# A two-layer network on one core: the scheduler's price for a change of array part, the experts' inputs transposed before their norm, and a twentieth place for weights

## The chip, the cores and the metric

The kernel runs on one core of a Trainium2 chip. The metric is the device time in microseconds, the median over runs of the same program. The engines go by the profile's names: PE (TensorE, with PEld for its weight loads), DVE (VectorE), ACT (ScalarE), POOL (GpSimd), SP (SyncE, which issues the DMAs).

## The reference

One sequence of 256 tokens of width 1024 goes through a first block (mixer and mixture of experts) and a second block of two layers. All is float32. Cut to what matters here:

```
h = rms_norm(x) * (1 + sc_m) + sh_m;  x = x + g_m * hybrid_mixer(h)     # SSD, forgetting attention, conformer
h = rms_norm(x, norm_ffn_g) * (1 + sc_f) + sh_f                          # the experts' inputs
e_logits, p_g = h @ w_re + b_re, softmax(h @ w_rg + b_rg)                # one of 4 groups, two of its 8 experts
y = sum over the two experts e of weight[e] * ((silu(h @ w_gate[e]) * (h @ w_up[e])) @ w_down[e])
x = rms_norm(x + g_f * y, final_norm_g)
for i in 0, 1:                                                           # the second block
    xn = rms_norm(x, norm_pre[i])
    y = rwkv7_time_mix(xn) if i == 0 else diff_attention_mix(xn, k, v)   # a recurrence per head, then attention
    x = x + rms_norm(y, norm_post[i])
    x = x + rms_norm(sigmoid(x @ ple_gate[i]) * (p[i] @ ple_w[i]), ple_norm[i])
```

`sc_f`, `sh_f` and the others are six parts of one modulation vector; `s.modc(n, j)` in the kernel is chunk j of part n, and part 3 is `sh_f`. There are 32 experts, each with 2 MB of gate, 2 MB of up and 2 MB of down weights: 192 MB in all. The recurrence of the time mix is done in chunks of 64 tokens, for which the inverse of a 64x64 triangular matrix is made per head.

## The kernel before

A dense product is made at float32 accuracy from three fast ones (type fp32r): each operand is split into a hi and a lo part, and hi·hi, hi·lo and lo·hi are added in PSUM. Small products and transposes are made in plain float32. A product with at most 64 rows of contraction or 64 output partitions uses a part of the 128x128 array. The diff writes a part as (rows, columns): (128, 128), (64, 64), (64, 128), (128, 64), (32, 32).

The work has three stages. In the mixer (`mixer_streams`, to L1118) and in the second block (`second`, L1524) the order of the instructions is made when the program is built: streams, which are generators that yield one instruction at a time, are merged by `Mux.run` (L317). `Plan` (L146 to 276) keeps for each engine the time at which it comes free, and for each tile the time at which it is ready. `Plan.cost` (L198) prices an instruction, `start` (L194) says when it can begin, `clocked` (L231) counts the work that TensorE is given in slots of 3413 ns and doubles a price where the slot before had little of it; `cool` (L242) says whether the recent work is under `HEAT`, and then `Mux.run` takes an fp32r product if one can go. `enter` (L248) books the instruction taken; there, an fp32r product behind one with at most 64 output partitions is priced 54 ns more. The plan is started anew for the second block (`reset`, L157).

The stage between them, the experts (`experts`, L1334), is ordered by hand: sixteen pairs of experts, the two of a pair in the two halves of the array's columns. For a pair the inputs of the tokens chosen are gathered by products with a 0/1 matrix `P` (`gather`, L1356: 32 products `px` per two pairs, evicted in four pieces of 128x512 by ScalarE and VectorE in turn), then `pgu` (gate and up), `ph` (transposes), `py` (down) and a scatter into `acc`. The weights come in pieces of 1 MB, by DMAs of SP's queue, into a ring of 19 places (`first_weights`, L1137): four of the pool `ring_b`, eleven tiles of their own (`MORE`), four of the pool `ring`. The places are taken from the mixer's memory, so that a load must wait for the mixer's last use of it, and all loads behind it on the queue wait with it. A place comes free again by the products that read it.

What the experts read, `hh` and `hl` (`s.h2`), is made at the end of the mixer. The stream `gather` (L1038, of the same name as the function above) makes `xc` = x * gain and sums squares, and from them the norm `rsq_y` (`s.rms2`, for each token one value on its partition). `tokens` (L1066) spreads the norm over all partitions as `R`, multiplies `xc` with it (eight times, `s.add`, VectorE or GpSimd) and adds `sh_f` (eight times, ScalarE). `turned` (L1080) then transposes `xc`, 128x128 at a time into four banks of PSUM, writes the hi part with ScalarE and the lo part with VectorE. Meanwhile `route` (L1246, tiles `qk`, `slot`, `wt`) chooses the experts, its sums over tokens being products with the triangular matrices `tri` and `stri`. `places` (L1345) makes `P` of `slot`.

In the second block, the names on TensorE are: `pd` dense fp32r products (of `xm`, the mixed inputs, in the time mix), `pi` the 64x64 and 32x32 products of `rwkv_invert` (L2242), `pm` and `pq` the transposes and products around it (`rwkv_inner`, L2123), `pe` those of `rwkv_chunks` (L2298). Eight pairs of heads go through inner, invert and chunks; in the invert each step of a pair is eight `pi` products, a copy on ScalarE, eight `pi` products, a copy and a transpose on VectorE. In the profile, all instructions of the two scheduled stages stand under L72, the helper that issues them.

Of the kernel before, what the change touches and what calls it, by code (L numbers as in the profile page):

```python
# [47 lines left out]
HEAT = 3500, 3550  # L48
# [3 lines left out]
MORE = 11  # L52
# [84 lines left out]
class Plan:  # L137
# [8 lines left out]
    def __init__(s, nc):  # L146
        s.nc = nc
        s.at = {}
        s.use = {}
        s.free = {}  # L150
        s.work, s.past, s.part, s.heat = {}, [], False, HEAT[0]
        s.log = []
        s.cur = None
        for n in ("tensor", "vector", "scalar", "gpsimd", "sync"):
            setattr(s, n, Lane(s, getattr(nc, n), n))

    def reset(s):  # L157

        s.at = {"dma": 0.0, "scalar": 10e3, "gpsimd": 11e3, "tensor": 16e3, "vector": 15.8e3}
        s.use, s.free, s.work, s.past, s.heat = {}, {}, {}, [], HEAT[1]  # L160
# [33 lines left out]
    def start(s, op, lag=0):  # L194
        eng = op.lane.name
        return op.ready if eng == "sync" else max(op.ready + lag * (eng == "tensor"), s.at.get(eng, 0.0))

    def cost(s, op):  # L198
# [4 lines left out]
        if eng == "tensor":  # L203
            if name == "transpose":
                return 109
            if ins[0].dtype == F32R:
                return max(107, n / 2.4) + 2
            m = out.ap[0][1]
            if m > 64:
                return max(214, n * 4 / 2.4 + 4)  # L210
            if s.box(out)[0]:
                return 22 if m <= 32 else 53
            return max(107, n * 4 / 2.4) + 2
# [16 lines left out]

    def clocked(s, start, dur, op):  # L231

        w = int(start / 3413.3)
        n = 1 if op.ins[0].dtype == F32R else 2
        for _, c in op.outs[0].ap[1:]:
            n *= c
        n *= op.ins[0].ap[0][1] / 128 * (dur > 53)
        s.work[w] = s.work.get(w, 0.0) + n
        s.past.append((start, n))
        return dur if s.work.get(w - 1, 0.0) > 3060 else 2 * dur  # L240

    def cool(s, t):  # L242

        while s.past and s.past[0][0] < t - 3413.3:
# [3 lines left out]
    def enter(s, op, r):  # L248
# [6 lines left out]
        else:  # L255
            start = s.start(op)
            if eng == "tensor":

                part = op.outs[0].ap[0][1] <= 64
                dur = s.clocked(start, dur + 54 * (s.part and op.ins[0].dtype == F32R), op)  # L260
                s.part = part
# [22 lines left out]
class Mux:  # L284
# [32 lines left out]
    def run(s):  # L317
        pl = s.plan
        while s.st:
# [10 lines left out]
            can = [(pl.start(o, x.lag), x.rank if o.lane.name == "tensor" else x.side, i, x, o) for i, x in enumerate(s.st) for o in x.head]  # L330
# [13 lines left out]
class K:  # L344
# [65 lines left out]
    def consts(s, tp):  # L410
# [18 lines left out]
        s.tri = cp.tile([128, 256], F32, name="tri")  # L429
# [3 lines left out]
        s.stri = cp.tile([128, 128], F32, name="stri")  # L433
# [39 lines left out]
    def mixer_streams(s, mp):  # L473
# [16 lines left out]
        for i in range(4):  # L490
            t("cu", S, tag=f"cu{i}")
        for i in range(2):
            for q in "hl":
                mp.tile([128, 8 * 268], F32R, name="w" + q, tag=f"w{q}{i}")
        t8 = t("t8", 8)
# [542 lines left out]
        def gather():  # L1038
# [12 lines left out]
            for j in range(NJ):  # L1051
# [3 lines left out]
                       A.activation(sq, xT[:, j], AF.Square)]  # L1055
                for c in range(2):
# [6 lines left out]
            s.pl = pl  # L1063
            done.add("rms")

        def tokens():  # L1066

            yield has("rms")
            tag = yield from s.one()
            R = s.bank(tag, [128, S])  # L1070
            yield from s.spread(s.rms2, R)
            yield A.copy(s.R1, R)
            s.give(tag)
# [6 lines left out]
        def turned(c):  # L1080
            for q in range(2):
                tag = yield from s.one()
                p = s.bank(tag, [128, 512])
                for j in range(4):
                    yield has(("x2", 4 * q + j))
                    yield nc.tensor.transpose(p[:, 128 * j:128 * j + 128], xc[:, 4 * q + j, 128 * c:128 * c + 128],
                                              ident)
                hi, lo = [x[:, c, 512 * q:512 * q + 512] for x in s.h2]
                yield A.copy(hi, p)
# [1612 lines left out]
```

## Time and profile before

| | us |
|---|---|
| median of three runs | 1298.44 (1293.02 to 1301.1) |
| the profiled execution | 1295.23, of which the span from first to last instruction 1293.3 |
| mixer, to the last expert input | 0 to some 221 |
| experts | some 221 to 662 |
| second block | 662 to 1293 |

The views of the trace are: the busy time of each engine; windows, which give the same for a stretch, with TensorE's granted clock (PEclk, 1.00 is 2.4 GHz and 0.50 is 1.2 GHz) and the DMA engines' share; and the timeline of one engine, in which neighbours of one kind stand in one row with their count. In a timeline the length of a row is that of the instructions from issue to end, and overlaps the next row's by the way through the engine: how long a run holds its engine is read from start to start.

### The profile page before, as it was taken

The page shows a single profiled execution, that of the slowest core. Times are in us where ns is not written, and L with a number is a line of the kernel's source. Part 1 is how long each engine was busy: PE and PEld are TensorE (multiplying, and loading weights), DVE is VectorE, ACT ScalarE, POOL GpSimd, SP SyncE. Part 2 cuts the span into 40 slices and gives each one's busy share as a digit, 9 for nine tenths or more (in the row PEclk, how much of TensorE's full clock was granted, in tenths as well). Part 3 has the DMA queues.
Part 4 walks back from the last instruction along what each step waited for, and adds up shares of the span by engine and source line. Part 5 has one row for each costly group of instructions (what it writes and reads, how often), then busy time and mean ns, then how long its engine had stood idle before and what let it go on. Part 6 is the DMA issues. An engine that isn't in the chain of part 4 may idle for free. (4 is left out here: it accounts for less than half of the span.)

```text
span 1293.3 us, 20461 instructions
## 1 busy us (share of the span) xinstructions
PE 1185.9 (92%) x7906; PEld 809.4 (63%) x7906; DVE 660.4 (51%) x1782; ACT 435.3 (34%) x1074; POOL 127.6 (10%) x358
## 2 busy tenths in 40 slices
PE   5999987999999989898986989999999989899896
PEld 3777886344343444444356867877777656888775
DVE  5695766111111111111027952576676677788885
ACT  3564543011110101111024721333344445655543
POOL 1000000000000000000000211222222002022212
PEclk8999996999999999999996975899999999899999
DMA  9658566899999999999983421111212342544422
GB/s 374 276 225 331 217 254 259 335 421 421 420 420 421 420 420 421 420 421 420 420 324 101 143 70 38 38 54 39 70 57 92 129 141 86 170 157 148 141 82 75
DMA packets 52628, 306.14 MB, mean 237 GB/s; under 512 B 5680, under 2 KB 10288, under 8 KB 25392
## 3 DMA queue, kind: packets, MB, share of 16 engines
q1 hardware_dynamic: 52368, 304.67, 60.1%
q8 instruction: 64, 1.05, 0.3%
q14 instruction: 36, 0.29, 0.1%
q0 software_dynamic: 160, 0.13, 0.1%
HBM read 302.55 MB, written 2.10 MB: 236 GB/s over the span
## 5 line engine op out<-in xcount | busy, mean ns | idle before, releaser
L366 PE MATMUL pgu<-w,xe 128*64 128x512 f32 x1024 | 233.0, 595 | 15.6 <-DMA w<-moe 15.6
L366 PEld LDWEIGHTS pgu<-w,xe 128*64 128x64 f32 x1024 | 80.9, 137 | 155.8 <-issue 116.6
L72 PE MATMUL pd<-xm,whl 128*128 128x256 f32 x768 | 149.3, 324 | 5.5 <-ACT xm L72 3.9
L72 DVE TENSOR_TENSOR whl<-raw,whl 128x512 fp32r<-128x512 f32 x192 | 128.4, 683 | 11.0 <-ACT whl L72 10.3
L72 ACT CAST whl<-raw 128x512 fp32r<-128x512 f32 x192 | 111.3, 618 | 40.5 <-PE pd L72 23.7
L72 PEld LDWEIGHTS pd<-xm,whl 128*128 128x128 f32 x768 | 112.9, 207 | 18.5 <-ACT xm L72 4.5
L366 PE MATMUL py<-w,hT 128*64 128x512 f32 (+1 forms) x528 | 116.6, 583 | 7.0 <-ACT hT L1408 7.0
L1433 DVE SCALAR_TENSOR_TENSOR yl<-py,ws,yh 128x512 fp32r<-128x512 f32 (+1 forms) x33 | 24.2, 734 | 123.4 <-ACT yh L1432 123.4
L366 PEld LDWEIGHTS py<-w,hT 128*64 128x64 f32 x528 | 40.7, 137 | 71.4 <-issue 54.7
L1352 POOL TENSOR_TENSOR PW<-P,wt 128x256 f32<-128x256 f32 x16 | 9.9, 617 | 617.7 <-PE pw L1413 213.4
L1432 ACT ACTIVATE yh<-py,ws 128x512 fp32r<-128x512 f32 (+1 forms) x33 | 22.2, 675 | 119.6 <-PE acc L366 66.1
L1398 DVE TENSOR_TENSOR hid<-hid,pgu 128x512 f32<-128x512 f32 x16 | 11.0, 688 | 98.2 <-PE pgu L366 98.1
L1397 DVE SCALAR_TENSOR_TENSOR hid<-hid,pgu 128x512 f32<-128x512 f32 x16 | 11.0, 688 | 96.8 <-ACT hid L1396 96.7
L72 PE MATMUL pd<-hh,whl 128*128 128x256 f32 x384 | 59.0, 295 | 1.4 <-ACT whl L72 0.8
L72 PE MATMUL pd<-xx,whl 128*128 128x256 f32 x384 | 54.2, 287 | 1.7 <-ACT whl L72 0.9
L72 PEld LDWEIGHTS pd<-hh,whl 128*128 128x128 f32 x384 | 50.6, 194 | 4.8 <-issue 2.6
L72 PE MATMUL pd<-whl,hh 128*128 128x512 f32 x192 | 52.4, 407 | 1.1 <-ACT hh L72 1.1
L72 PEld LDWEIGHTS pd<-xx,whl 128*128 128x128 f32 x384 | 48.9, 192 | 3.5 <-ACT whl L72 1.2
L72 PE MATMUL a<-hl,wh 128*128 128x256 f32 x160 | 47.1, 294 | 1.5 <-DVE hl L72 1.5
L72 PE MATMUL a<-hh,wh 128*128 128x256 f32 x160 | 46.8, 292 | 0.6 <-DVE x L72 0.6
L72 PE MATMUL a<-hh,wl 128*128 128x256 f32 x160 | 46.5, 291 | 0.0
L72 DVE TENSOR_TENSOR wl<-w,wh 128x512 fp32r<-128x512 f32 (+1 forms) x60 | 39.3, 692 | 10.5 <-ACT wh L72 10.4
(506 smaller groups left out, 2230.3 us busy)
## 6 DMA issues: line engine op xcount, KB each, us to landing
w<-moe SPq DMA_DIRECT2D x190, 1024.0 KB, 19.8
w<-ada SPq DMA_DIRECT2D x12, 2048.0 KB, 11.8
raw<-awin SPq DMA_DIRECT2D x32, 512.0 KB, 3.4
raw<-bwin SPq DMA_DIRECT2D x32, 512.0 KB, 3.5
w<-win SPq DMA_DIRECT2D x5, 2048.0 KB, 12.0
raw<-pleg SPq DMA_DIRECT2D x16, 512.0 KB, 3.3
w<-wout SPq DMA_DIRECT2D x2, 2048.0 KB, 8.6
raw<-awout SPq DMA_DIRECT2D x8, 512.0 KB, 3.4
```

Of the source, the lines that this page charges most:

```text
L72: r = s.fn(*s.a, **s.k)
L366: return s.nc.tensor.matmul(out, lhsT=lhsT, rhs=rhs, start=first, stop=last, **kw)
L1352: G.tensor_tensor(PW.rearrange(four, e=2), P[:, :, o:o + 128].bitcast(F32).rearrange(four, e=2), wt[:, :, 2 * i:2 * i + 2, None].to_broadc ...
L1397: V.scalar_tensor_tensor(hid, hid, 1.0, pgu[0], op0=OP.add, op1=OP.mult)
L1398: V.tensor_tensor(hid, hid, pgu[1], op=OP.mult)
L1432: A.activation(y[0], p, AF.Copy, scale=ws)
L1433: V.scalar_tensor_tensor(y[1], p, ws, y[0].bitcast(F32), op0=OP.mult, op1=OP.subtract)
```

## The change

The change has three parts.

The planner. A change between parts of the array is priced (`change`: 95 ns, 138 where little work was booked in the slot before; nothing within a part, and nothing from (64, 128) to (128, 128)) and is part of the time at which a product can start. `come`, by which streams are compared, leaves the price out once the present spell of one kind (fp32r or not) has lasted `LONG`. The prices of the small products and the work booked for them go by part, and `HEAT` is another.

```
-HEAT = 3500, 3550
+SPELL = 3413.3
+WORK = {(128, 128): 3.2, (64, 64): 1.7, (64, 128): 2.2, (128, 64): 1.9, (32, 32): 1.5, (128, 32): 1.0}
+HEAT = 3300, 3300
+LONG = 400, 1400
-MORE = 11
+MORE = 12
...
     def start(s, op, lag=0):
         eng = op.lane.name
-        return op.ready if eng == "sync" else max(op.ready + lag * (eng == "tensor"), s.at.get(eng, 0.0))
+        if eng == "tensor":
+            return max(op.ready + lag, s.at.get(eng, 0.0) + s.change(op))
+        return op.ready if eng == "sync" else max(op.ready, s.at.get(eng, 0.0))
+
+    def come(s, op, lag=0):
+        t = s.start(op, lag)
+        if op.lane.name == "tensor":
+            at = s.at.get("tensor", 0.0)
+            if at - s.since > (LONG[s.whole]):
+                t = max(op.ready + lag, at)
+        return t
...
+    def cold(s, t):
+        return s.work.get(int(t / SPELL) - 1, 0.0) < 2880
+
+    def change(s, op):
+        op = getattr(op, "ops", [op])[0]
+        if s.part is None or s.part == s.form(op) or (s.part, s.form(op)) == ((64, 128), (128, 128)):
+            return 0
+        return 138 if s.cold(s.at.get("tensor", 0.0)) else 95
+
     def clocked(s, start, dur, op):
-        w = int(start / 3413.3)
-        n = 1 if op.ins[0].dtype == F32R else 2
+        part, whole = s.form(op), op.ins[0].dtype == F32R
+        cold = s.cold(start)
+        if cold:
+            dur = 2 * (dur - 11) if whole else 1.9 * dur
+        if whole and part != s.part:
+            dur += 165 if cold else 105
+        n = 1.0 if whole else 1.5 if op.op == "transpose" else WORK[part]
...
-            can = [(pl.start(o, x.lag), x.rank if o.lane.name == "tensor" else x.side, i, x, o) for i, x in enumerate(s.st) for o in x.head]
+            can = [(pl.come(o, x.lag), x.rank if o.lane.name == "tensor" else x.side, i, x, o) for i, x in enumerate(s.st) for o in x.head]
```

The experts' inputs. `tokens` is gone. `turned` transposes `xc` without its norm, as soon as its chunks are made; the norm, which then lies along the partitions, is the scale of the eviction that makes the hi part, and of the one that makes the lo part. `sh_f` is added where the gathered inputs leave PSUM, for which each bank is evicted in two pieces.

```
-        def tokens():
...
-            for j in range(NJ):
-                x = xc[:, j]
-                yield s.add(x, x, s.R1, OP.mult, 150)
-                yield A.activation(x, x, AF.Identity, bias=s.modc(3, j))
-                done.add(("x2", j))
...
+            tags, ps = [], []
+            for q in range(2):
+                yield has(*[("x2", 4 * q + j) for j in range(4)])
+                tags.append((yield from s.one()))
+                ps.append(s.bank(tags[q], [128, 512]))
+                for j in range(4):
+                    yield nc.tensor.transpose(ps[q][:, 128 * j:128 * j + 128], xc[:, 4 * q + j, 128 * c:128 * c + 128],
+                                              ident)
             yield has("rms")
             for q in range(2):
...
+                rs = s.rms2[:, c:c + 1]
+                yield A.activation(hi, ps[q], AF.Copy, scale=rs)
+                yield V.scalar_tensor_tensor(lo, ps[q], rs, hi.bitcast(F32), op0=OP.mult, op1=OP.subtract)
+                s.give(tags[q])
...
-                (V.tensor_copy if q % 2 else A.copy)(xe[:, 2 * q:2 * q + 2], p)
+                for j in range(2):
+                    sh = s.modc(3, 2 * q + j)
+                    if q % 2:
+                        V.tensor_scalar(xe[:, 2 * q + j], p[:, j], sh, None, op0=OP.add)
+                    else:
+                        A.activation(xe[:, 2 * q + j], p[:, j], AF.Identity, bias=sh)
```

The memory. A twelfth tile of its own makes twenty places. For it `stri` and `tri` become one tile `order`, which later holds the weighted matrix `PW`; `hid` and `hT` use the memory of `condp`; and some of the mixer's tiles (`R1`, `xc`, `dg`, `wr36`) are made in another order, so that the last places lie under other tiles than before.

On VectorE, at the end of the mixer, these were the last rows ahead of `P` (`xc` the multiplications by the norm, `qk`, `wt`, `slot`, `cnt` the routing, `hl` the lo parts of the experts' inputs):

```order
L72 TENSOR_TENSOR xc<-xc,R_196 128x256
L72 TENSOR_TENSOR wt<-qk 128x64
L72 SCALAR_TENSOR_TENSOR slot<-x_2271,qk 128x64
L72 TENSOR_TENSOR hl<-x_229,hh 128x512
L72 TENSOR_SCALAR slot<-slot 128x64
L72 TENSOR_TENSOR hl<-x_230,hh 128x512
L72 TENSOR_REDUCE qk<-x_2271 128x1
L72 CAST cnt<-qk 128x1
L72 TENSOR_TENSOR hl<-x_2294,hh 128x512
L72 TENSOR_TENSOR hl<-x_2303,hh 128x512
L1345 TENSOR_TENSOR P<-slot,iot 128x512
```

These are they now, from the first lo part on, and, behind ten more rows of the routing, down to `P`:

```order
L76 SCALAR_TENSOR_TENSOR hl<-x_2216,rsq_y,hh 128x512
L76 SCALAR_TENSOR_TENSOR qk<-qk 128x64
L76 SCALAR_TENSOR_TENSOR hl<-x_2136,rsq_y,hh 128x512
L76 TENSOR_REDUCE qk<-qk 128x8
L76 SCALAR_TENSOR_TENSOR hl<-x_2217,rsq_y,hh 128x512
```

```order
L76 TENSOR_TENSOR wt<-qk 128x64
L76 SCALAR_TENSOR_TENSOR slot<-x_2283,qk 128x64
L76 TENSOR_SCALAR slot<-slot 128x64
L76 TENSOR_REDUCE qk<-x_2283 128x1
L76 CAST cnt<-qk 128x1
L1388 TENSOR_TENSOR P<-slot,iot 128x512
L1411 TENSOR_SCALAR xe<-px,mod 128x256 x4
```

The four `hl` rows (the fourth stands among the routing's rows further up) have moved ahead of the routing's second half, and no row of `xc` is left between.

On TensorE, in the second block, where the invert of a pair of heads begins (`pi` its products, `pd` the dense ones, `pm` and `pq` those of the pairs before their invert; the numbers are those of tiles), the rows were:

```order
L72 MATMUL pd_5713<-xm_4945,whl 128x256 x2
L72 MATMUL pi_5804<-T,PQ 64x64
L72 MATMUL pd_5713<-xm_4945,whl 128x256
L72 MATMUL pi_5804<-T,PQ 64x64 x7
L72 MATMUL pq<-AR,BK 128x128
L72 MATMUL pd_5713<-xm_4945,whl 128x256 x3
L72 MATMUL pi_5804<-Gt,T 64x64 x5
L72 MATMUL pd_5713<-xm_4945,whl 128x256
L72 MATMUL pi_5804<-Gt,T 64x64
```

and in the corresponding place they are now:

```order
L76 MATMUL pi_5790<-T,PQ 64x64 x8
L76 MATMUL pm<-ident,rkv 128x128 x2
L76 MATMUL pd_5721<-xm_4918,whl 128x256 x8
L76 MATMUL pm<-ident,BK 128x128 x4
L76 MATMUL pi_5790<-Gt,T 64x64 x8
L76 MATMUL pi_5831<-T,PQ 64x64 x8
L76 MATMUL pd_5721<-xm_4918,whl 128x256 x3
L76 MATMUL pm<-la,whl 128x256
L76 MATMUL pd_5721<-xm_4918,whl 128x256 x3
L76 MATMUL pm<-la,whl 128x256 x3
L76 MATMUL pd_5721<-xm_4918,whl 128x256
L76 MATMUL pi_5861<-T,PQ 64x64 x8
```

Where eight `pi` products were taken one and seven, or five and one by one, they stand in eights, and the `pd` products in runs of three and more.

On TensorE in the middle of the mixer, `orow` (rows of the attention's output; their transposes are the last readers of the memory into which the fifth expert weight is loaded) and `dta` (the SSD's decays) stood so, among the conformer's products `a`, about fifty rows ahead of the first `yr` (the SSD's output):

```order
L72 MATMUL a_1713<-wh,hh 128x256
L72 MATMUL a_1713<-wl,hh 128x256
L72 MATMUL x_1724<-tri,dta 128x128 x4
L72 MATMUL x_1726<-ident,orow 128x128 x2
L72 MATMUL a_1713<-wh,hl 128x256
```

and now, behind the first `yr`:

```order
L76 MATMUL x_1866<-ident,yr 128x128 x2
L76 MATMUL x_1874<-ident,yr 128x128 x2
L76 MATMUL x_1882<-ident,orow 128x128
L76 MATMUL a_1857<-hh,wh 128x256
L76 MATMUL x_1882<-ident,orow 128x128
```

The transposes of `orow` have moved behind those of the first `yr`; the last two of them follow fourteen rows further on.

## Rows read from the trace of the kernel before

**Rows 1.** The page, part 1: busy us (share of the span) x instructions.
```profile
PE 1185.9 (92%) x7906; PEld 809.4 (63%) x7906; DVE 660.4 (51%) x1782; ACT 435.3 (34%) x1074; POOL 127.6 (10%) x358
```

**Rows 2.** Stages: window, length, then busy us (instructions) of PE, PEld, DVE, ACT, POOL; PEclk; DMA share; GB/s.
```profile
0.00:207.00 207.00, 184.49 (x1332) 149.84 (x1332) 136.63 (x416) 100.24 (x245) 5.79 (x16) 0.97 0.69 277
...
232.00:662.00 430.00, 406.60 (x2037) 181.46 (x2034) 69.51 (x114) 47.07 (x75) 9.25 (x15) 1.00 1.01 419
...
690.00:755.00 65.00, 53.35 (x386) 49.06 (x387) 59.45 (x149) 35.13 (x86) 12.28 (x28) 0.89 0.43 141
...
770.00:821.00 51.00, 51.00 (x308) 38.12 (x305) 15.89 (x43) 9.93 (x26) 3.38 (x13) 0.50 0.11 34
...
836.00:994.00 158.00, 154.68 (x1601) 122.39 (x1600) 109.37 (x317) 54.25 (x143) 41.81 (x165) 1.00 0.18 58
```

**Rows 3.** Timeline of DVE, hand-over: start, length, line, operation, count, [idle before <-releaser].
```profile
208.56 0.16 DVE L72 SCALAR_TENSOR_TENSOR rsq_y<-rsq_t,rsq_y 128x2 f32<-128x2 f32 x1
...
211.79 0.42 DVE L72 TENSOR_TENSOR xc<-xc,R 128x256 f32<-128x256 f32 x1
212.12 0.22 DVE L72 TENSOR_TENSOR qk<-qk 128x64 f32<-128x64 f32 x1
...
218.66 0.69 DVE L72 TENSOR_TENSOR hl<-x,hh 128x512 fp32r<-128x512 f32 x1 [0.45 <-ACT hh L72]
219.51 0.69 DVE L72 TENSOR_TENSOR hl<-x,hh 128x512 fp32r<-128x512 f32 x1 [0.16 <-ACT hh L72]
220.12 0.68 DVE L1345 TENSOR_TENSOR P<-slot,iot 128x512 fp32r<-128x512 f32 x1
```

**Rows 4.** Timeline of SP's queue: the first and the later loads of expert weights.
```profile
147.26 21.71 SPq L391 DMA_DIRECT2D w<-moe  x8
...
231.34 18.08 SPq L391 DMA_DIRECT2D w<-moe  x10
```

**Rows 5.** Windows of 5 us around the restart, columns as in rows 2.
```profile
225.00:230.00 5.00, 5.00 (x27) 3.44 (x28) 1.12 (x2) 0.59 (x1) 0.00 (x0) 0.79 0.00 0
```

**Rows 6.** Timeline of PE: the first gather's products and the first expert products.
```profile
220.95 0.55 PE L366 MATMUL px<-P,hh 128*128 128x256 f32 x1 [2.09 <-DVE P L1345]
...
227.66 13.95 PE L366 MATMUL pgu<-w,xe 128*64 128x512 f32 x64
```

**Rows 7.** Timeline of PE in the mixer: transposes of orow and yr.
```profile
157.12 0.38 PE L72 MATMUL x<-ident,orow 128*128 128x128 f32 x2
...
169.49 0.72 PE L72 MATMUL x<-ident,yr 128*128 128x128 f32 x4 [2.02 <-DVE yr L72]
```

**Rows 8.** Timeline of PE in the invert stretch, at full clock: runs of products.
```profile
856.33 0.74 PE L72 MATMUL pd<-xm,whl 128*128 128x256 f32 x4
857.00 0.32 PE L72 MATMUL pi<-T,PQ 64*64 64x64 f32 x2
857.26 0.39 PE L72 MATMUL pd<-xm,whl 128*128 128x256 f32 x1
857.57 0.33 PE L72 MATMUL pi<-T,PQ 64*64 64x64 f32 x4
857.84 0.93 PE L72 MATMUL pq<-AR,BK 64*128 64x128 f32 x6
858.70 0.68 PE L72 MATMUL pi<-Gt,T 64*64 64x64 f32 x16
859.31 0.38 PE L72 MATMUL pd<-xm,whl 128*128 128x256 f32 x1
859.62 0.49 PE L72 MATMUL pq<-AR,BK 64*128 64x128 f32 x2
860.04 0.85 PE L72 MATMUL pd<-xm,whl 128*128 128x256 f32 x5
```

**Rows 9.** Timeline of PE in the low stretch: a single pd product, a run of seven.
```profile
772.65 0.58 PE L72 MATMUL pd<-xm,whl 128*128 128x256 f32 x1
...
814.41 1.86 PE L72 MATMUL pd<-xm,whl 128*128 128x256 f32 x7
```

More of the change, by code (lines that the diff above doesn't have):

```diff
@@ L150, in __init__ @@
         s.free = {}
-        s.work, s.past, s.part, s.heat = {}, [], False, HEAT[0]
+        s.work, s.past, s.part, s.heat, s.whole, s.since = {}, [], None, HEAT[0], False, 0.0
         s.log = []
@@ L159, in reset @@
         s.at = {"dma": 0.0, "scalar": 10e3, "gpsimd": 11e3, "tensor": 16e3, "vector": 15.8e3}
-        s.use, s.free, s.work, s.past, s.heat = {}, {}, {}, [], HEAT[1]
+        s.use, s.free, s.work, s.past, s.part, s.heat, s.whole, s.since = {}, {}, {}, [], None, HEAT[1], False, 0.0
     def __getattr__(s, x):
@@ L229, in pointers, with form @@
         return sum(isinstance(v, bass.AP) for v in x)
-    def clocked(s, start, dur, op):
-        w = int(start / 3413.3)
-        n = 1 if op.ins[0].dtype == F32R else 2
+    @staticmethod
+    def form(op):
+        if op.op == "transpose":
+            return 128, 128
+        return tuple(128 if n > 64 else 64 if n > 32 else 32 for n in (op.ins[0].ap[0][1], op.outs[0].ap[0][1]))
+    def cold(s, t):
[5 more added lines that the diff above has]
+        return 138 if s.cold(s.at.get("tensor", 0.0)) else 95
+    def clocked(s, start, dur, op):
+        part, whole = s.form(op), op.ins[0].dtype == F32R
[5 more added lines that the diff above has]
+        n = 1.0 if whole else 1.5 if op.op == "transpose" else WORK[part]
         for _, c in op.outs[0].ap[1:]:
             n *= c
-        n *= op.ins[0].ap[0][1] / 128 * (dur > 53)
-        s.work[w] = s.work.get(w, 0.0) + n
+        w, end = int(start / SPELL), start + dur
+        behind = max(0.0, min(1.0, (end - (w + 1) * SPELL) / dur))
+        s.work[w] = s.work.get(w, 0.0) + n * (1 - behind)
+        s.work[w + 1] = s.work.get(w + 1, 0.0) + n * behind
         s.past.append((start, n))
-        return dur if s.work.get(w - 1, 0.0) > 3060 else 2 * dur
+        if whole != s.whole:
+            s.whole, s.since = whole, start
+        s.part = part
+        return dur
     def cool(s, t):
-        while s.past and s.past[0][0] < t - 3413.3:
+        while s.past and s.past[0][0] < t - SPELL:
             s.past.pop(0)
@@ L257, in enter @@
             if eng == "tensor":
-                part = op.outs[0].ap[0][1] <= 64
-                dur = s.clocked(start, dur + 54 * (s.part and op.ins[0].dtype == F32R), op)
-                s.part = part
+                dur = s.clocked(start, dur, op)
             end = start + dur
@@ L494, in mixer_streams @@
                 mp.tile([128, 8 * 268], F32R, name="w" + q, tag=f"w{q}{i}")
+        t("xc", 8, S)
+        for i in range(4):
+            t("dg", 128, tag=f"dg{i}")
+        t("wr36", 8, 36)
         t8 = t("t8", 8)
@@ L1392, in inner, with room, hidden @@
             return pgu
-        def hidden(pgu, tag="hid"):
-            hid = e2.tile([128, 512], F32, name="hid", tag=tag)
+        def room(own):
+            return e2.tile([128, 8, 256], F32, name="room", tag="xe")[:, :2].rearrange("p k n -> p (k n)") if own else \
+                s.condp.rearrange("p a b c -> p (a b c)")
+        def hidden(pgu, own=False):
+            hid = room(own)
             A.activation(hid, pgu[0], AF.Tanh, scale=0.5)
```

66 lines of the change are left out of this document (29 added, 37 removed).

## The prediction

> **What bounds the kernel now.** I read the busy times first, then busy time by stage, then the stages that change. VectorE is busy for half of the span, TensorE for 92% of it [rows 1], so the question is what binds each stage. The stage windows [rows 2] part the span in three. Up to 207 us (the mixer) TensorE has 184 of 207 us, the rest being waits in chains. From 232 to 662 us, the experts, the DMA share is 1.01 at 419 GB/s: the 1 MB weight pieces (1,048,576 bytes / 419 GB/s = 2.50 us each) set the time, and what TensorE, VectorE or ScalarE do there is free. In the second stage's heart TensorE is busy for all 51 us of 770 to 821 and for 154.7 of the 158 us to 994: its products, and what it loses between them, are the time. In 770 to 821 us its granted clock is 0.50, the lower level (1.2 GHz), so 51 us pass for 25.5 us of work at 2.4 GHz.
>
> Between mixer and experts lies a hand-over that the whole stream of weights waits for. SP issues ten loads in a row only from 231.34 us [rows 4]: its 19 places are full until the first expert products free one. In 225 to 230 us nothing is moved at all [rows 5]. Each microsecond by which the first `pgu` product starts sooner is one off the end, and so is a place that is filled before it.
>
> **The hand-over.** VectorE is its path [rows 3]. From `rsq_y` (208.56) to `P` (220.12), which the gather's products wait for, it does the routing (`qk`), eight multiplications of `xc` by the spread norm, and the four lo parts. The multiplications are issued 8 times, and each delays the row behind it by 0.33 us (211.79 to 212.12): 8 x 0.33 = 2.6 us. They go. The four lo parts stay (now scalar_tensor_tensor, 0.6 us start to start), but move ahead, between routing steps, because the transposes no longer wait for the norm; the 0.45 and 0.16 us of waiting for ScalarE's hi parts go. Together 3.2 us; nothing where the routing's own products (`qk,order`) come late. I take 3.0, for the ten `qk` rows between stay dependent on one another. The 32 gather products then take 6.7 us, from 220.95 to `pgu` at 227.66 [rows 6]; I leave that as it is. The eight evictions per gather instead of four lie inside the DMA-bound stretch, where VectorE has 70 of 430 us and ScalarE 47 [rows 2]: free there. In the first gather alone they are exposed, but the first `pgu` product needs only the first of them; without that cover it would be some 0.4 us, an `xc` row of the same 128x256 [rows 3].
>
> The twentieth place: one piece fewer is moved after the restart, 2.5 us, if it arrives before. It does if SP keeps up. Load 5 and all behind it on SP's queue wait for the transposes of `orow`, which free its place. In before the last of these ran at 157.12, and the first eight loads were issued from 147.26 on; the first `yr` transposes ran at 169.49 [rows 4, 7]. Now the last `orow` pair stands behind those of `yr`, so load 5 can't go before about 175; I allow 186. Then 15 pieces x 2.5 = 37.5 us end at 223.5, before the restart at some 228: cost nothing. If it came later than 190 us, each microsecond would be lost. Hand-over together: -5.5 us, ends -5.7 and 0.
>
> **The changes of array part.** The order of TensorE's instructions in the second stage has the same 3244 products, but 331 changes between parts of the array instead of 540. Visits to (128,128) runs fall from 236 to 116, visits to fp32r runs behind a smaller part from 187 to 78, runs of smaller parts by 89. What a visit costs [rows 8]: a run of four `pd` products holds TensorE from 856.33 to 857.00, a run of one from 857.26 to 857.57; so 0.36 us / 3 = 0.12 per product, and 0.31 - 0.12 = 0.19 us for the visit itself. A run of sixteen `pi` products takes 0.61 (858.70 to 859.31), one of two 0.26: 0.025 per product, and 0.21 for the visit. So 109 fewer fp32r visits are 109 x 0.19 = 20.7 us, and 89 fewer small ones 89 x 0.20 = 17.8. The upper bound is 38.5. The lower is 20.7, if a small visit's 0.2 us is only the first product's way through the array, which other work would fill. I take 30, the middle. No other engine hides it: in these stages TensorE is the row that is full [rows 2].
>
> The Trainium skill, TensorEngine Tiling (Array Packing), Key Properties, says that a change of tiling mode drains TensorE. It gives no figure. By it the planner's free step from (64,128) to (128,128) isn't free. The trace agrees: six `pq` products take 0.86 us (857.84 to 858.70), two in front of a (128,128) run 0.42 (859.62 to 860.04), so 0.11 each and 0.20 for the visit, as with the others. The new order has 45 such `pq` runs instead of 52, so its free step costs it no more than before, and the sum stands.
>
> What the longer runs cost: a head's chain (`pi`, ScalarE's copy, `pi`, VectorE's copy and transpose, and again) must wait while a long `pd` run goes through. As several heads' chains stand one behind the other now (8 `pi`, 8 `pi`, then `pd`), I put new stalls at +3 us, between 0 and 10: before, 836 to 994 us holds 3.3 us of idle TensorE.
>
> **The clock.** In 770 to 821 us `pd` products came in ones to fours between small ones [rows 9]; a run of seven stood at 814.41, and the clock was up at 821. From 836 to 994 us it was 1.00 [rows 2]. In the new order the fp32r products of this stretch, from the first `pi` to the first `pe`, come in 5 runs of 10 on average instead of 30 of 2.1, and the planner books each part's work by a table. If the stretch is not low at all, 25.5 us come back; if it is as long as before, none. I take 14, just over half, since such runs are what stood ahead of the return.
>
> **Mixer.** 125 changes in both orders, the same products: 0, with 4 us to either side for moved chains.
>
> **The sum.** The profiled run took 1295.23 us (span 1293.3 and 1.9 around it). 1295.2 - 5.5 - 30 + 3 - 14 = 1248.7. The median of the three runs shown stands 3.2 higher, so 1252.
>
> **The rivals.** A, as above: 0.66. Its own range: 1237 to 1268.
> B, the clock falls in the invert stretch as before and as long: the other terms alone, 1295.2 - 5.5 - 30 + 3 + 3.2 = 1266. For it: the stretch before it, 690 to 755 us, has 0.89 already [rows 2], and the products are the same; against it: the longer runs. 0.20.
> C, the chains become the bound: fewer visits mean fewer chances for a chain's next step. Eight pairs of heads with some 16 such hops each, every one held up by a visit's 0.2 us, make 128 x 0.2 = 26 us, and TensorE, idle in pieces, doesn't regain the clock: 1295.2 - 5.5 - 30 + 26 + 3.2 = 1289. Against it: two pairs are in the invert at a time and a third in its chunks, so one fills the other's wait. 0.08.
> D, slower: the long runs gather the dense products in a few places and leave pockets of small ones, and the low clock that ended at 821 lasts on towards 940. 119 us at half speed cost 60 us: 1295.2 - 5.5 - 30 + 3 + 60 + 3.2 = 1326. It undoes the gain from 65 us more of low clock, and makes it slower by over 1% from 91. For it: the clock of 836 to 994 held at 1.00 with fp32r products every microsecond or two [rows 2, 8]. Against it: the planner puts an fp32r product in when its own count of work is low. 0.06.
> The Trainium skill, TensorE: Matmul & The Clock Gate, A second HAM failure mode, tells of a kernel whose clock swung between its two levels because TensorE idled briefly between groups. Here that is the way to B and C; in the trace of before the low stretch had TensorE busy for all of its 51 us [rows 2], so brief idling isn't what showed there.
>
> **How the numbers follow.** About 1% (13 us) is what a measurement of this kernel can tell from no change. A and B lie below 1285.5 (0.86), C mostly within 1% (0.06, and 0.02 below), D above (0.05, and 0.01 within): faster 0.88, same 0.07, slower 0.05. The 80% range takes A's lower end with the 38.5 and some more clock, 1232, and reaches over B to C's edge, 1286.
>
> **What would show it.** The first `pgu` some 3 us sooner, and the restart of SP's loads with it; all 20 loads issued ahead of it. Stage 232 to 662 shifted, not shortened beyond 2.5 us. TensorE's busy time in the second stage down by about 44 us with 331 changes. Granted clock in the invert stretch above 0.7. I'm wrong on the clock if a stretch of 0.50 as long as 50 us stands there, and wrong on the changes if the products' busy time is the same and idle time has grown.

## The result, and the profile after

The changed kernel takes 1250.68 us (median of 4, 1249.09 to 1252.17), the kernel before 1298.02 in the runs beside it: 0.9639 of its time, 95% interval 0.9606 to 0.9672. The profiled execution took 1252.17 us, its span is 1250.4. The forecast was 1252. Executions of one program differ mostly by how long TensorE has the low clock (the changed kernel's four by 3 us; those of the kernel before by up to 25, from 1291.46 at a mean clock of 0.952 to 1316.28 at 0.928), so stages are compared with their clock beside them, and medians and ratios leave out executions more than 1.5% above their program's fastest.

The windows of both traces, cut at the same events (first `px`, last expert product, first `pd` product, first `pi`, last `pe`, first and last product of the attention's dense part, end), with the columns of [rows 2]. First the kernel before:

```profile
220.95:682.94 461.99, 435.31 (x2184) 202.69 (x2184) 79.31 (x132) 58.25 (x103) 9.87 (x16) 0.98 0.97 401
682.94:692.12 9.18, 3.06 (x12) 2.71 (x12) 4.88 (x19) 3.69 (x11) 0.64 (x4) 0.50 0.36 118
...
754.83:1053.07 298.24, 292.27 (x2658) 222.80 (x2658) 183.61 (x539) 105.35 (x268) 54.59 (x205) 0.90 0.22 71
1053.07:1097.53 44.46, 40.85 (x163) 28.08 (x162) 30.77 (x84) 23.38 (x61) 8.11 (x5) 0.96 0.20 70
1097.53:1225.91 128.38, 117.04 (x912) 108.06 (x911) 108.16 (x262) 75.03 (x215) 23.21 (x78) 0.97 0.46 152
1225.91:1293.30 67.39, 52.44 (x239) 40.69 (x239) 47.16 (x127) 27.98 (x73) 13.10 (x6) 0.97 0.26 87
```

and the changed kernel:

```profile
220.79:678.76 457.97, 432.17 (x2184) 198.98 (x2184) 78.25 (x142) 56.92 (x103) 9.84 (x16) 0.99 0.98 402
678.76:690.53 11.77, 3.06 (x13) 2.71 (x12) 8.57 (x26) 9.32 (x27) 0.64 (x4) 0.50 0.30 106
...
755.37:1002.90 247.53, 241.32 (x2655) 195.89 (x2654) 180.31 (x539) 105.64 (x270) 51.66 (x205) 0.96 0.26 86
1002.90:1050.34 47.44, 40.69 (x157) 29.36 (x157) 30.71 (x84) 22.55 (x60) 8.29 (x5) 0.89 0.18 61
1050.34:1187.60 137.26, 120.85 (x915) 110.28 (x913) 109.79 (x264) 75.43 (x217) 25.20 (x78) 0.96 0.41 143
1187.60:1250.40 62.80, 51.37 (x237) 39.47 (x236) 45.59 (x125) 27.67 (x71) 11.31 (x6) 0.95 0.26 92
```

| stage | before | after | difference |
|---|---|---|---|
| mixer, to the first gather product | 220.95 | 220.79 | -0.2 |
| experts | 461.99 | 457.97 | -4.0 |
| from the last expert product to the first of the time mix | 9.18 | 11.77 | +2.6 |
| time mix ahead of the first invert | 62.71 | 64.84 | +2.1 |
| time mix, invert and chunks | 298.24 | 247.53 | -50.7 |
| end of the first layer | 44.46 | 47.44 | +3.0 |
| attention | 128.38 | 137.26 | +8.9 |
| end of the second layer | 67.39 | 62.80 | -4.6 |

One stage gives more than the whole, and the others give 8 us of it back. In that stage TensorE is as full as before (6.0 us idle before, 6.2 after), with the same products. From the trace's records: changes of part 495 before, 286 after; visits to fp32r runs behind another part 167 and 59; low clock 59.4 us and 20.5 us (PEclk 0.90 and 0.96). The low time that is gone, 38.9 us, is worth at most half of it, 19.5. The other 31.2 us are left for the changes, some 34 with the embedding products (`pi<-ple`, sixteen instead of eleven, 8.4 us instead of 5.5) that the stage now holds besides. This is a remainder and not a measurement; the prices of the rows (0.093 us a change, and 0.105 more where it leads to an fp32r run) give 209 x 0.093 + 108 x 0.105 = 30.8.

The timeline of TensorE there shows the new runs, to be held against [rows 8] and [rows 9]:

```profile
772.02 1.58 PE L76 MATMUL pd<-xm,whl 128*128 128x256 f32 x11
773.53 0.68 PE L76 MATMUL pi<-T,PQ 64*64 64x64 f32 x16
774.05 0.63 PE L76 MATMUL pi<-Gt,T 64*64 64x64 f32 x16
...
775.75 1.33 PE L76 MATMUL pd<-xm,whl 128*128 128x256 f32 x9
```

Eleven `pd` products hold TensorE for 1.51 us (772.02 to 773.53), 0.12 each and 0.19 for the visit: the prices are the old ones, only the visits are fewer. Sixteen `pi` products go by in one run, 0.52 us to 774.05.

The hand-over on VectorE, for [rows 3]:

```profile
209.77 0.16 DVE L76 SCALAR_TENSOR_TENSOR rsq_y<-rsq_t,rsq_y 128x2 f32<-128x2 f32 x1
...
210.88 0.75 DVE L76 SCALAR_TENSOR_TENSOR hl<-x,rsq_y,hh 128x512 fp32r<-128x512 f32 x1
...
213.54 0.74 DVE L76 SCALAR_TENSOR_TENSOR hl<-x,rsq_y,hh 128x512 fp32r<-128x512 f32 x1
...
214.34 0.74 DVE L76 SCALAR_TENSOR_TENSOR hl<-x,rsq_y,hh 128x512 fp32r<-128x512 f32 x1
...
215.12 0.74 DVE L76 SCALAR_TENSOR_TENSOR hl<-x,rsq_y,hh 128x512 fp32r<-128x512 f32 x1
...
218.16 0.23 DVE L76 SCALAR_TENSOR_TENSOR slot<-x,qk 128x64 f32<-128x64 f32 x1
...
219.53 0.19 DVE L76 TENSOR_REDUCE qk<-x 128x1 f32<-128x32 f32 x1 [0.93 <-PE x L76]
...
219.95 0.69 DVE L1388 TENSOR_TENSOR P<-slot,iot 128x512 fp32r<-128x512 f32 x1
```

and on TensorE, for [rows 6]:

```profile
220.79 0.55 PE L411 MATMUL px<-P,hh 128*128 128x256 f32 x1 [1.29 <-DVE P L1388]
...
227.50 7.95 PE L411 MATMUL pgu<-w,xe 128*64 128x512 f32 x36
```

From the last `rsq_y` to the first `px` product it is 11.02 us instead of 12.39. The multiplications and the waits for ScalarE are gone, but VectorE now stands 0.93 us in front of the count (`qk<-x` at 219.53), and the lo parts stand between the routing's steps. The norm itself ended 1.2 us later, so that nothing of the 1.4 us is seen at `px`. A difference of that size comes with the execution: in the profile of e7 below, which is the same program up to the second layer, the last `rsq_y` stands at 207.51 instead of 209.77, and the first `px` at 218.53. SP's loads restart at 231.17 [rows 4].

### The profile page after: what moved, and what is told of

It reads as the page before. It is cut to its first block, busy times and chain, and to the rows that moved or that the text cites. A ratio compares the mean times of both kernels' runs of the same rounds, so it can differ in the third digit from the quotient of the medians.

```text
span 1250.4 us, 20460 instructions
## 1 busy us (share of the span) xinstructions
PE 1136.9 (91%) x7902; PEld 783.9 (63%) x7902; DVE 656.9 (53%) x1790; ACT 434.5 (35%) x1081; POOL 124.3 (10%) x358
## 5 line engine op out<-in xcount | busy, mean ns | idle before, releaser
L76 PE MATMUL pd<-xm,whl 128*128 128x256 f32 x768 | 122.5, 307 | 8.0 <-ACT xm L76 6.5
L411 PE MATMUL py<-w,condp 128*64 128x512 f32 x480 | 108.4, 596 | 7.0 <-ACT condp L1461 7.0
L76 PEld LDWEIGHTS pd<-xm,whl 128*128 128x128 f32 x768 | 105.7, 205 | 13.6 <-ACT xm L76 7.1
L411 PEld LDWEIGHTS py<-w,condp 128*64 128x64 f32 x480 | 35.8, 137 | 69.2 <-issue 55.0
L1395 POOL TENSOR_TENSOR order<-P,wt 128x256 f32<-128x256 f32 x16 | 9.8, 615 | 615.3 <-PE pw L1466 419.5
L1451 DVE TENSOR_TENSOR condp<-condp,pgu 128x512 f32<-128x512 f32 x15 | 10.3, 687 | 97.6 <-PE pgu L411 97.6
L1450 DVE SCALAR_TENSOR_TENSOR condp<-condp,pgu 128x512 f32<-128x512 f32 x15 | 10.3, 688 | 95.3 <-ACT condp L1449 95.3
L76 PE MATMUL pd<-xx,whl 128*128 128x256 f32 x384 | 58.2, 290 | 1.9 <-ACT whl L76 1.1
```

Of the source, the lines that this page charges most:

```text
L76: r = s.fn(*s.a, **s.k)
L411: return s.nc.tensor.matmul(out, lhsT=lhsT, rhs=rhs, start=first, stop=last, **kw)
L1395: G.tensor_tensor(PW.rearrange(four, e=2), P[:, :, o:o + 128].bitcast(F32).rearrange(four, e=2), wt[:, :, 2 * i:2 * i + 2, None].to_broadc ...
L1450: V.scalar_tensor_tensor(hid, hid, 1.0, pgu[0], op0=OP.add, op1=OP.mult)
L1451: V.tensor_tensor(hid, hid, pgu[1], op=OP.mult)
```

## The experiments

**Which part of the change.** First the changed kernel with the scheduler of before, then the kernel before with the new one. Each takes the class `Plan` and the constants of the other kernel whole; of the choice the first one's edit is

```
-            can = [(pl.come(o, x.lag), x.rank if o.lane.name == "tensor" else x.side, i, x, o) for i, x in enumerate(s.st) for o in x.head]
+            can = [(pl.start(o, x.lag), x.rank if o.lane.name == "tensor" else x.side, i, x, o) for i, x in enumerate(s.st) for o in x.head]
```

and the second one's the reverse.

> The changed kernel with the scheduler of before: the second block's order is that of before (540 changes of array part), so only the new place and the experts' inputs are left of the change. Theory P (the planner's order carries all but the place): the twentieth place takes 2.5 us off and the hand-over some 0.2, so 1294 to 1297 us, the invert stage as long as before (298 us). Rival Q (the inputs and the place carry the 5.5 us that I forecast, the shift of the norm merely hides it): 1291 to 1293.

> The kernel before with the new planner alone; the second block's order has 331 changes, as in the changed kernel. Theory P: 1252 to 1256 us, the changed kernel plus the place's 2.5 us. Rival Q: the hand-over and the place are worth 5.5 us, so 1256 to 1259.

The first took 1310.5 us (ratio to before 1.0088, 1.0035 to 1.0141), the second 1251.61 (0.9622, 0.9563 to 0.968). So the scheduler carries all of the gain, P, but P's price for the rest was wrong too: inputs and place alone make the kernel slower. In the profile of the first the experts are 4.1 us shorter, the invert stage 3.2 us longer (301.4, low clock 66.7 instead of 59.4), and the stretch from the last expert product to the first `pd` 19.6 us instead of 9.2. With the new scheduler alone that stretch is 9.18 us.

**The place.** The changed kernel with 19 places:

```
-MORE = 12
+MORE = 11
```

> The changed kernel with 19 places instead of 20. Theory Y (the last place lies on memory that the second block's first weights need, so it gives its 2.5 us back there): the experts' stage 2.5 us longer, the stretch from the last expert product to the first product of the time mix 9.2 us as before instead of 11.8, the total within 1 us of 1250.7. Rival Z (the stretch is longer for another reason, the tiles that were merged): 11.8 us still, and 1253.

1247.92 us (0.9578, 0.9512 to 0.9645). The experts are 460.24 us, 2.3 longer than with 20 places, and the stretch behind them 9.15 instead of 11.77: Y, though the total is 2.8 us off 1250.7 and not within 1. The activities of ScalarE show what the place costs. With 20 places:

```profile
675.37 0.83 ACT L1212 ACTIVATE w<-x 128x256 f32<-128x256 f32 x2 [2.08 <-DVE x L1548]
679.38 0.83 ACT L1212 ACTIVATE w<-x 128x256 f32<-128x256 f32 x2 [3.18 <-DVE x L1548]
680.40 3.21 ACT L76 CAST whl<-raw 128x512 fp32r<-128x512 f32 x6 [0.19 <-ACTq L1231]
683.52 3.92 ACT L76 ACTIVATE wm<-w,vec 128x64 f32<-128x64 f32 x16
```

With 19:

```profile
670.71 1.14 ACT L76 CAST whl<-raw 128x512 fp32r<-128x512 f32 x2
...
673.72 1.64 ACT L76 CAST whl<-raw 128x512 fp32r<-128x512 f32 x3
...
676.78 2.00 ACT L76 ACTIVATE wm<-w,vec 128x64 f32<-128x64 f32 x8
...
680.66 1.52 ACT L76 ACTIVATE wm<-w,vec 128x64 f32<-128x64 f32 x6
682.09 1.12 ACT L76 CAST whl<-raw 128x512 fp32r<-128x512 f32 x2
```

The splits of the second block's first weights (`whl`, `wm`) ran in ScalarE's waits during the last experts; with the twentieth place they stand behind the end of the stage (`<-ACTq L1231`, its branch for overflow). That the place lies on their memory is what I take for the cause; which tiles collide wasn't tried. Nor was it tried why the same place cost 10 us with the old scheduler, where the first of the second block's loads in a row was issued only at 683.15, and here at 669.02.

**The price of a change against the count of work.** Four kernels: the price left out of the choice; the price kept, but a count like that of before; the count alone put into the kernel before; and the changed kernel without the forcing of fp32r products.

The first (e3), in `change`, with `start` for `come` in the choice:

```
-        return 138 if s.cold(s.at.get("tensor", 0.0)) else 95
+        return 0
```

the second (e4), in `clocked`, with HEAT = 3500, 3550 and 3060 for 2880:

```
-        n = 1.0 if whole else 1.5 if op.op == "transpose" else WORK[part]
+        n = 1.0 if whole else 2.0
...
+        n *= op.ins[0].ap[0][1] / 128 * (part[0] == 128 or part[1] == 128)
```

the third (e9), in `clocked` of the kernel before, with HEAT = 3300, 3300:

```
-        n = 1 if op.ins[0].dtype == F32R else 2
+        n = 1.0 if op.ins[0].dtype == F32R else 1.5 if op.op == "transpose" else WORK[s.form(op)]
...
-        n *= op.ins[0].ap[0][1] / 128 * (dur > 53)
...
-        return dur if s.work.get(w - 1, 0.0) > 3060 else 2 * dur
+        return dur if s.work.get(w - 1, 0.0) > 2880 else 2 * dur
```

and the fourth (e10):

```
-HEAT = 3300, 3300
+HEAT = 0, 0
```

> The changed kernel with the price of a change of part taken out of the choice (change gives 0, come is start); the new prices of small products and the new count of work stay. The order has 412 changes and 142 visits to fp32r runs from a smaller part instead of 331 and 78. Theory A (the changes cost what the rows show): (412 - 331) x 0.093 + (142 - 78) x 0.105 = 14 us more than the changed kernel, 1262 to 1268 us with the clock as in the changed kernel, up to 19 more if the low stretch is back. Rival B (what was won is the clock, by the new count of work): the changed kernel's 1250 within 5 us, with the clock as high.

> The changed kernel with the price of a change, but with the count of work and the thresholds of before (two for any product that is not fp32r, by its rows, none for those with both sides small; HEAT 3500 and 3550). The order has 381 changes and 76 visits. Theory A with the clock following the long runs: (381 - 331) x 0.093 = 5 us more than the changed kernel, 1253 to 1258 us, low clock in the invert stage some 20 us as now. Rival B (the count of work is what keeps the clock up): low clock of 50 us and more, and 1268 to 1276 us.

> The kernel before, in which only the planner's count of work is changed (the table by array part, HEAT 3300, the threshold 2880); prices, choice, memory and experts' inputs are those of before. The order comes out with 388 changes and 127 visits to fp32r runs instead of 540 and 187, with no price on a change at all. Theory C (the count does both: the planner no longer believes that TensorE idles while small products run, so it breaks in with fewer fp32r products and spreads them over the stage): low clock in the invert stage 25 us or less, the stage 250 to 262 us, the total 1255 to 1270. Rival A (the price and the new durations are needed too): low clock above 45 us, the stage above 275, the total above 1278.

> The changed kernel with HEAT = 0: no fp32r product is ever put in because recent work is low; the count is left to do no more than set the planner's own durations. The order has 327 changes and 73 visits, next to the 331 and 78 of the changed kernel. Theory C': with the right count the forcing is hardly ever asked for, and the clock is kept by the spread of the dense products: low clock in the invert stage within 10 us of the changed kernel's 20, the total 1247 to 1256. Rival H (the forcing at the right moments is what holds the clock): low clock of 45 us and more, the total above 1262.

| kernel | price | count | changes, fp32r visits (invert stage) | low clock | invert stage | median | ratio to before |
|---|---|---|---|---|---|---|---|
| before | no | old | 495, 167 | 59.4 | 298.2 | | |
| e4 | yes | old or less | 336, 57 | 114.9 | 305.5 | 1307.98 | 1.0049 (1.0012 to 1.0086) |
| e9 | no | new | 345, 108 | 57.6 | 264.8 | 1250.62 | 0.9623 (0.9579 to 0.9666) |
| e3 | no, new durations | new | 366, 121 | 17.1 | 251.5 | 1255.86 | 0.968 (0.9574 to 0.9786) |
| e10 | yes | new, no forcing | 282, 54 | 35.3 | 256.2 | 1258.99 | 0.9687 (0.9642 to 0.9731) |
| after | yes | new | 286, 59 | 20.5 | 247.5 | 1250.68 | 0.9639 (0.9606 to 0.9672) |

(Lengths in us, of the profiled execution; that of e9 was the longest of its five, 1267.2, the others 1249.4 to 1253.7.)

e4 decides whether the price is enough. It has fewer fp32r visits than the changed kernel (57 and 59) and 10.3 products to a visit where that has 10.0, and it is no faster than before: B, and slower than B's 1268 to 1276. Its windows and groups show what happens:

```profile
834.00:930.00 96.00, 91.98 (x994) 76.81 (x993) 64.84 (x186) 36.91 (x96) 22.65 (x82) 0.94 0.24 78
930.00:1035.00 105.00, 96.25 (x803) 70.76 (x801) 54.23 (x178) 29.66 (x81) 15.83 (x77) 0.61 0.14 43
```

```profile
L76 PE MATMUL pd<-xm,whl 128*128 128x256 f32 x480 | 74.8, 303 | 0.0
```

All 480 dense products of the time mix are done by 921 us, 54% of the stage (in the changed kernel at 78%, 948.6 us). In the 105 us from 930 on TensorE works on small products (of some 800 records about 50 are fp32r), with 9 us of idle time, and the granted clock is 0.61. That is my rival D, in a kernel with the price and without the new count. e4 books nothing at all for a product with both sides at most 64, so its planner takes a stretch of `pi` products for idleness and calls for fp32r products until there are none. The kernel before is a shade less blind, as it books 64 for those of them that begin at partition 0 (the new count books 109 for each); there the calls make single `pd` products [rows 9], and with the price, long runs too early. This is read from the code and the orders; no run takes it apart. As e4's count is the cruder of the two, it shows the direction, and its 115 us aren't what the price with the very count of before would have. Nor does it show why the clock fell in the kernel before: there the low stretch, to 821 us, stands among `pd` products, the last of which comes at 81% of the stage (997.6 us), no earlier than in the changed kernel.

e9 shows the other side: the count alone (the table with its thresholds), without a price, takes visits from 167 to 108 and reaches the time of the whole change, below C's 1255 to 1270.

```profile
755.98:1020.75 264.77, 260.00 (x2649) 210.24 (x2648) 178.31 (x536) 102.25 (x264) 52.81 (x205) 0.89 0.23 73
```

Against C, its low time in the profiled execution is as long as before, 57.6 us; the stage is 33 us shorter all the same. The mean clock of that execution was 0.950, that of the four others 0.961 to 0.966, and they were 14 to 18 us shorter. So the visits saved stay, but the low clock of one and the same order varies by tens of us, and the count alone doesn't always keep it away. e10 is neither C' nor H: without the forcing there are 15 us more of low clock and 4 us more of idle time, and the total is 8 us longer.

On what the price is worth beside the count, e3 and the changed kernel differ by 4.0 us in the stage where 14 were expected. The visits do cost what the rows showed (medians of records from start to start, in both: 0.120 within an fp32r run, 0.223 for its first product, 0.209 for its last, so 0.19 a visit), but the stages don't hold the same work: the changed kernel does sixteen embedding products of 0.6 us in it (8.4 us), e3 three (1.6). With them it is some 11 us. In the whole e3 is 5 us slower, between A and B, with intervals that overlap. By the same measure e9, without the new durations, is no slower than the changed kernel.

**The hand-over.**

The count's sums in a bank of their own, ahead of `slot`, and the lo parts held back:

```
+        tag2 = yield from s.one()
+        pc = s.bank(tag2, [128, 3, 32])
+        yield s.mm(pc[:, 0], s.ones, oh[:, 0], True, False)
+        yield s.mm(pc[:, 0], s.ones, oh[:, 1], False, True)
...
-        yield s.mm(pp[:, 2], s.ones, oh[:, 0], True, False)
-        yield s.mm(pp[:, 2], s.ones, oh[:, 1], False, True)
```

```
                 yield A.activation(hi, ps[q], AF.Copy, scale=rs)
+            yield lambda: len(s.top) > 1
```

> The changed kernel with the sums for the count of tokens per expert (two products of qk and order) in a bank of PSUM of their own, so that they needn't wait until slot has been read out of the first. Theory S (a wait took the place of the one removed: the count's, 0.93 us on VectorE right ahead of P): from the end of the norm (last rsq_y) to the first px product 10.1 us instead of 11.0, the total 0.9 us less, which the times can't tell from 1250.7. Rival T (the chain of the routing's steps ahead of slot sets P): 11.0 as now.

> The changed kernel with the four lo parts held back until the routing is at its last step, so that they no longer stand between its steps on VectorE. Theory S (each lo part of 0.66 us between the steps delays the chain, and behind it they would fill the waits of the last steps): from the last rsq_y to the first px product 9.5 to 10 us instead of 11.0. Rival T (between the steps they filled waits, and behind them they only add): 11.5 to 12.5. Of the total 1 us either way.

From the last `rsq_y` to `px`: 10.49 us with the count's own bank, 10.95 with the lo parts late, 11.02 in the changed kernel and in the others with its inputs (six profiles, 11.01 or 11.02). The count's wait was there and cost 0.5 us, not 0.9: S in kind, half in size. The place of the lo parts makes no difference, neither S nor T. 1250.35 and 1252.06 us in all, nothing that could be told from 1250.68.

**The second layer.** From the moment at which the attention's streams are added, `cost`, `clocked` and `cool` are those of before, and `change` gives 0:

```
+            s.plan.old = True
             s.diff(yT)
```

> The changed kernel, in which the planner goes back to the rules of before from the second layer on (differential attention and the two last parts around it); the time mix keeps its new order. Theory W (the new order gives 7 us back there, at the wait ahead of each head's transpose of its output, now 1.3 to 2.1 us, before 1.0 to 1.3): from the end of the time mix to the end of the span 240 to 242 us instead of 247.5, the total 1243 to 1246. Rival X (these 7 us are the granted clock, low for 27 us there instead of 15, whatever the order): 245 to 249 us, the total 1248 to 1252.

1246.75 us (0.9574, 0.951 to 0.9638). The three last stages are 46.98 + 129.81 + 65.38 = 242.2 us, against 247.5: W, just outside its range. The total alone couldn't tell it: e5, e6 and e8, measured beside it, have ratios of 0.958 to 0.9601 with intervals that overlap. The groups of TensorE in the attention, for the transposes of each head's output (the last columns are idle time ahead of them); kernel before, changed kernel, and this one:

```profile
L72 PE MATMUL pi<-ident,on 128*128 128x128 f32 x12 | 2.5, 287 | 6.8 <-DVE on L72 6.8
```

```profile
L76 PE MATMUL pi<-ident,on 128*128 128x128 f32 x12 | 2.5, 287 | 10.5 <-DVE on L76 10.5
```

```profile
L77 PE MATMUL pi<-ident,on 128*128 128x128 f32 x12 | 2.5, 286 | 6.8 <-DVE on L77 6.8
```

The order that suits the time mix costs 3.7 us at this wait alone. In all three the number of changes in the attention is 28, so here the new price had nothing to win.

**A version of the parts that paid.** Old rules in the second layer, 19 places and the count's own bank; and the same without the price in the time mix:

The first (c1) has the edits of e5, e7 and MORE = 11, the second (c2) that of e3 besides.

> A version put together from the runs: the changed kernel with the planner's rules of before from the second layer on, 19 places, and the count's sums in a bank of their own. If the parts add up: 1250.7 - 5 (second layer) - 0.5 (hand-over) - 0 to 2 (the place and its price in memory): 1243 to 1246 us; if the second layer's gain was chance, 1248 to 1250.

> The mixed version again, with the price of a change out of the choice in the time mix too (412 changes and 142 visits instead of 331 and 79), so that its order comes from the new count and the new durations alone. Theory A (each visit saved is worth what its rows show, though part of it falls into waits): the invert stage 4 to 14 us longer than the mixed version's 248, the total 1247 to 1257 against 1243.2. Rival B (all is in the count, the price is worth nothing): 1241 to 1245 us.

c1 takes 1243.23 us (median of 6, 1238.25 to 1253.31; 0.956, 0.9522 to 0.9598): faster than before, and by its ratio than the changed kernel (0.9606 to 0.9672). Its three last stages are 245.2 us in its longest execution, which is the one profiled. c2 takes 1257.63 (0.9629, 0.9577 to 0.968), its invert stage 256.5 us against 248.3: A, the total 0.6 us above its range. So on top of the count and the new durations the price is worth some 9 us by the ratios, whose intervals just overlap.

## Why the prediction was right

The total was 1252 against 1250.7, and case A is what happened. By its steps:

- The changes of part: forecast -30 (20.7 to 38.5). In the invert stage 31 to 38 us are left for them beside the clock, from 108 fewer fp32r visits and 209 fewer changes, at prices that are the same in both traces and give 30.8; the rest of the remainder is not explained. Right, and for the reason given, though the upper bound priced a small visit too high: the last product of a `pi` run takes 0.148 us where one within it takes some 0.035, so a visit costs 0.11 and not 0.20, and 109 x 0.19 + 89 x 0.11 = 30.5. The trace has some 4350 records of TensorE in the second stage, not 3244; its 540 and 331 changes are those forecast.
- The clock: forecast -14 (0 to 25.5), in the profiled pair -16 to -19.5 in that stage (38.9 us of low time, by the ratio of records below or by half). The size was near, the reason isn't borne out. I took longer runs of fp32r products to be what brings the clock back; e4 has 10.3 products to a visit and 115 us of low clock, once its dense products are used up, and e3 has 4.9 and 17.1 us. The runs that have the new count have 14 to 35 us, but for e9's profiled execution. Why the clock fell from 770 to 821 us in the kernel before and not in the changed one, no run shows apart, as the count alters order and visits together. I named the table of work in half a sentence and put no number on it, though it was the part of the planner that decided, over the visits as well (e9).
- New stalls: forecast +3 (0 to 10) in the time mix, measured +0.2 there. They came in the attention instead, where I had looked for nothing: +8.9 us, of which e7 shows 7 to be the new order's.
- The hand-over: forecast -3.0 (0 to 3.2), measured -1.4 by its own events; at `px` the profiled pair can't tell it from the difference of two executions. The eight multiplications went, but a chain of dependent routing steps with TensorE at the low clock in it stays, and the count's wait (0.5 us by e5) took a part of their place. I summed VectorE's busy time where the chain set the pace.
- The twentieth place: forecast -2.5, measured -2.6 at the last `py` (670.95 and 668.38), and 2.6 us given back at the next stage's first weights (e8). The other 1.6 us by which the experts are shorter are not the place's: from the last `py` to the stage's end it is 11.99 us before and 10.38 after, but 10.39 in e8 with 19 places. I followed the loads ahead of the experts, not the memory behind them. The delayed `orow` transposes cost nothing, as forecast: load 5 (counted from 0, so the sixth of the queue, not the fifth) was issued at 176.21 (I allowed 186), the twentieth at 210.34, the restart came at 231.17.
- The mixer: 0 forecast, -0.2 measured, with the hand-over in it.

So errors cancelled: hand-over and place gave 3.9 us less than forecast, stages to which I had given nothing lost 2.1 and 7.3, and the time mix gained 9.7 more (50.7 instead of 41). From profile to profile the forecast was 46.5 us and 43.1 were measured; that the medians agree within 2 us is partly luck, as the 3.2 us by which the kernel before was above its profile were added to the forecast, while the changed kernel's median is 1.5 us below its own. Rival B was wrong on the clock, C on the chains of the time mix. D's mechanism exists (e4). The argument I gave against D, that the planner puts an fp32r product in when its count is low, is only a part of what keeps the changed kernel from it: without that (e10) the low time is 35 us, far from D's.

The Trainium skill, TensorE: Matmul & The Clock Gate, A second HAM failure mode, tells of a kernel whose clock swung between its levels because TensorE idled briefly between groups of products. Here idling isn't needed: the trace of before has low clock with TensorE busy for 51 of 51 us [rows 2] and no idle time in the 7 us ahead of the fall at 770, and in the changed kernel the falls at 790 and 916 us follow 7 us with at most 0.03 us of it. In e4 1.0 us of idle time stands in the 7 us ahead of the fall at 930, so there it may have had a part.

## What to carry to other kernels

A list scheduler orders the work for the machine that its cost table describes: when an order is bad, ask first what the table says of the instructions in that stretch, before adding a rule to the choice. Here a class of small products counted as little or no work, and a new count alone, with its thresholds, was worth as much as the whole change. And a saving made ahead of a stage boundary is worth what the next stage's first instruction sees of it: a place more for weights, taken, as I read it, from memory that the next stage needs, moved 2.6 us and saved none.

## What the runs showed that I had not expected

The number of changes doesn't hang on a price alone: with the old count the planner made 167 visits to fp32r runs, many of one product, and with the new count and no price on a change they fell to 108 by themselves.

At the low clock records take 1.7 to 1.8 times as long, not twice, as the prediction's 25.5 of 51 us has it: 0.213 us against 0.119 within an fp32r run, 0.378 against 0.223 for its first product (medians from start to start in the kernel before). Half the low time is therefore the upper end of what a stage loses by it.
